# A decoder trunk on one core: later planner slots for the first scores of each pair of heads and for the norms' third block of transposes

## The chip, the cores and the metric

The kernel runs on one core of one Trainium2 chip. The metric is the device time of one execution in microseconds; the three runs of the kernel before lie between 1220.03 and 1221.92, with a median of 1221.85.

## The reference, cut to what matters

Two layers over a residual stream x of 512 tokens by 1024 features, all in float32:

```python
for l in range(2):
    h = x @ w_in[l]
    (fq, fk, fv, fgate, cq, ckv, kr, sq, sk, sv, wq, wk, wv) = split(h)
    out_a = causal_softmax(heads(fq), heads(fk), heads(fv), bias=cumsum(log_sigmoid(fgate + b)))
    out_b = mla(cq, ckv, kr, ...)            # low-rank q and kv, rotary key
    out_c = stick_breaking(heads(sq), heads(sk), heads(sv))
    out_d = sliding_window(heads(wq), heads(wk), heads(wv), sinks, slopes)
    y = group_rmsnorm(concat([out_a, out_b, out_c, out_d])) @ w_o[l]
    x = layernorm(ALPHA * x + y, ln1_g[l], ln1_b[l])
    f = (silu(x @ w_gate[l]) * (x @ w_up[l])) @ w_down[l]
    x = layernorm(ALPHA * x + f, ln2_g[l], ln2_b[l])
```

Each of the four groups has 4 heads of 64; the scores of groups A, B and C are causal, group D looks 128 tokens back.

## The kernel before, in words

The 512 tokens form four blocks of 128 (`NT` = 4, `t` from 0 to 3). x lies token by token (tile `x_res`); for the projections it is also held feature by feature (tile `xT`), which TensorE makes by transposing 128x128 pieces. Every float32 product is made as three products of a high and a low part (high x high, high x low, low x high), so operands exist in pairs: a high part, mostly a cast on ScalarE (L722, L453, L927), and a low part, the difference, on VectorE or GpSimd (L442, L444). One step over 128 of the summed features, with its three matmuls, is called a slice here; a projection chunk has eight. In the profile the weights' parts are named w_hi and w_lo, or qk where they borrow those buffers.

**How the order is made.** When the program is built, a planner (class `Sched`, L120 to L201) lays every operation out in estimated time. A generator asks for a slot with `Op(engine, cost, dep)`; `dep` holds, for each engine, the estimated time at which operands made there are done. The earliest start is the engine's free time or the operands' times plus a hand-over (`NEAR`), whichever is later. `pick` looks at all requests that wait for an engine, takes those whose start is within 30 ns (`SLACK`) of the earliest, and of these the one of the best priority. `mark(e, t)` makes a `dep` that says "ready on engine e at time t". The estimates set only the order in which each engine gets its instructions, and which PSUM bank or which of two engines is taken; on the chip each engine runs its list in that order, and semaphores make it wait for true operands. `sums` already asks for its slot 1500 ns behind its operand in this way.

**Scores.** `causal_group` (L1515 on) makes the heads of groups C, A and B. For each head h it makes three requests b = 0, 1, 2 through `head`: b = 0 is key blocks 0 and 1 (in the order, rows of 128x128, 128x256 and a mask row 128x2x128), b = 1 is 384 wide, b = 2 is 512 wide. All three read the same q and k (`operands(h)`). A pair of heads (0 and 1, 2 and 3) shares one q tile and one k tile. `head` asks for its score slot on TensorE and makes the scores; `normed` turns them into weights on ScalarE, VectorE and GpSimd; then come transposes of the weights (L1558), their evacuation to tile pt, and with the third the product with the values.

**Norms.** `layernorm` (L793 on) works through one token block t: statistics (L811 to L841, and L477 to L481 on tile lnst), a centred product (L854), and the final scale and shift in two halves of 512 columns (L859), all on VectorE. Ahead of them L1744 (first norm) or L2004 (second) adds the residual. When a half is done, `transpose_x(t, h, dep)` asks for four transposes of it on TensorE (L752); ScalarE and VectorE evacuate them to xT (L453, L442). The second norm of the last layer writes the output and transposes nothing, so there are three such places: the first norm of layer 0, its second norm, and the first norm of layer 1. While the last blocks are normed, TensorE has the next projection's slices for the first blocks to do. `load_x` uses `transpose_x` too, for the input.

Of the kernel before, what the change touches and what calls it, by code (L numbers as in the profile page):

```python
# [32 lines left out]
NT = S // P  # L33
# [32 lines left out]
E_PE, E_ACT, E_DVE, E_POOL, E_SP = range(5)  # L66
# [11 lines left out]
def join(*deps):  # L78

    if any(x is None for x in deps):  # L80
        return None
    return tuple(map(max, zip(*deps))) if len(deps) > 1 else deps[0]


def mark(e, t):
    return NOW[:e] + (t,) + NOW[e + 1:]
# [22 lines left out]
def c_mm(n):  # L109
    return max(107.0, 0.4225 * n)  # L110
# [9 lines left out]
class Sched:  # L120
# [9 lines left out]
    def spawn(self, gen, prio=0, order=None):  # L130
        self.n += 1
        self.step((gen, prio, self.n if order is None else order), None)
# [220 lines left out]
def trunk(ctx: ExitStack, tc: tile.TileContext, d):  # L353
# [43 lines left out]
    ident = const.tile([P, P], F32, name="ident")  # L397
    x = const.tile([P, NT, D], F32, name="x_res")
    x_dep = [None] * NT
# [7 lines left out]
    given = {"const": Joint(4)}  # L407
# [333 lines left out]
        return u, e  # L741


    def transpose_x(t, h, dep, then=None, keep=None):

        def half():
            yield lambda: r_u.ready()
            u = r_u.take()
            e = yield Op(E_PE, 4 * 107.0, join(u.dep, dep))
            for k in range(4):  # L750
                kk = h * 4 + k
                PE.transpose(out=u.tile[:, k * P:(k + 1) * P], in_=x[:, t, kk * P:(kk + 1) * P], identity=ident)  # L752
            tok = slice(t * P, (t + 1) * P)
            dst = [xt["t"][:, h * 4:h * 4 + 4, a, tok] for a in range(2)]
            e2 = yield from evac(dst, u.tile.rearrange("p (k n) -> p k n", k=4), S, join(e, xt["dep"]))
            if keep:
                e3 = yield from keep(h, tok, u.tile.rearrange("p (k n) -> p k n", k=4), e)
                u.give(join(e2, e3))
            else:
                u.give(e2)  # L760
            both = turned_x.setdefault(t, Joint(2))
            both.add(join(e, e2))
            if both.dep:
                xT_at[t] = turned_x.pop(t).dep
                if then:
                    then(t, both.dep)

        spawn(half())
# [98 lines left out]
    def layer(l):  # L867
# [602 lines left out]
        def mixf_ready(g, ticket):  # L1470
            return NOW if g in mixfs else mixf_turn.ready(ticket)

        def take_mixf(g):
            if g not in mixfs:
                mixfs[g] = mixf_turn.take()
# [39 lines left out]
        def causal_group(g, operands, extras, strict, normed, values, v_at, n_work, free_qk):  # L1515

            ticket = mixf_turn.ticket()
            heads = Joint(4, lambda dep: spawn(finish(g, dep)))
            extras = extras or (lambda h, i, o: [])

            def masks(o, b):

                if b == 0:
                    return o.rearrange("p (a n) -> p a n", a=2)[:, :, :P], identb, maskb[:, strict:strict + 1].broadcast_to([P, 2, P])
                return o[:, (b + 1) * P:(b + 2) * P], identb, maskb[:, strict]

            out = []
            for h in range(4):
                turned = Joint(3)
                pts = {}  # L1530
                pt_ticket = pt_turn.ticket()

                def head(b, ps, w, h=h, turned=turned, pts=pts, pt_ticket=pt_ticket):
                    blocks = ((0, 1), (1, 2)) if b == 0 else ((b + 1, b + 2),)
                    pairs, dep = operands(h)
                    cost = 108.0
                    for i, n in blocks:
                        cost += len(pairs) * c_mm(n * P)
                        for _, _, y in extras(h, i, ps.tile[:, :n * P]):
                            cost += max(54.0, 0.4225 * y.shape[-1])  # L1540
                    e = yield Op(E_PE, cost, join(dep, ps.dep, given["const"].dep))
                    c = 0
                    for i, n in blocks:
                        o = ps.tile[:, c:c + n * P]
                        qk_mm(o, pairs, i, n * P, c == 0, [masks(ps.tile, b)] * (c == 0) + extras(h, i, o))
                        c += n * P
                    free_qk(h, e)
                    p, end = yield from normed(ps, blocks, w, e)

                    yield lambda: join(r_u.ready(), NOW if pts else pt_turn.ready(pt_ticket))  # L1550
                    if not pts:
                        pts["pt"] = pt_turn.take()
                    pt = pts["pt"]
                    u = r_u.take()
                    n = 3 if b < 2 else 4
                    e = yield Op(E_PE, 107.0 * n, join(u.dep, end))
                    for k in range(n):
                        PE.transpose(out=u.tile[:, k * P:(k + 1) * P], in_=p.tile[:, k * P:(k + 1) * P], identity=ident)  # L1558
                    p.give(e)
                    e = join(e, pt.dep)  # L1560
                    e = yield from evac_blocks(pt.tile, u.tile, PIECES[b], e)
                    u.give(e)
                    turned.add(e)
                    if turned.dep is None:
                        return

                    ready = yield lambda: join(at[v_at].dep, r_u.ready(), mixf_ready(g, ticket)) if v_at in at else None
                    take_mixf(g)
                    v = v_of[values].tile
                    o = r_u.take()  # L1570
                    e = yield Op(E_PE, 2 * 600.0, join(turned.dep, ready, o.dep))
                    for kb in range(NT):
                        s0 = PLACE[kb] + kb
                        for part in range(2):
                            mm(o.tile[:, kb * P:], v[:, kb, h, :, :].rearrange("p a c -> p (a c)"),
                               pt.tile[:, part, s0 * P:(s0 + NT - kb) * P], start=(kb == 0 and part == 0), stop=False)
                    pt.give(e)
                    v_uses[values].add(e)
                    heads.add((yield from merge(o, g, h, e)))

                for b in range(3):
                    out.append((lambda h=h: operands(h) and operands(h)[1], n_work, lambda ps, w, b=b, head=head: head(b, ps, w)))
            return out
# [597 lines left out]
    def load_x(*ts):  # L2181
        def loads():
            for t in ts:
                x_dep[t] = yield from dma(x[:, t], d["x"][0, t * P:(t + 1) * P, :], 1.46)
                for h in range(2):
                    transpose_x(t, h, join(x_dep[t], given["ident"]), scale_x)
        return loads

    def first():
# [83 lines left out]
```

## Time and profile before

| | |
|---|---|
| median of three runs | 1221.85 us |
| profiled execution | 1222.01 us |
| its span | 1220.2 us (1.8 us lie around it) |
| TensorE busy | 1182.5 us, 7589 matmuls |
| VectorE, ScalarE, GpSimd busy | 896.0, 680.2, 247.6 us |
| mean granted TensorE clock | 0.992 |

How to read it: PE is TensorE, DVE VectorE, ACT ScalarE, POOL GpSimd. A row of the timeline has the start, the duration, engine, line, operation, and in brackets the engine's idle time before it with the operation that ended it. Neighbouring rows may be joined (x4 is four instructions), and matmuls overlap at their ends, so durations of neighbours add up to more than the time they take. A row of the table by stretches has the stretch, its length, busy time with the count of instructions for TensorE, its weight loads, VectorE, ScalarE and GpSimd, then the granted clock as a share of full speed, the share of DMA time and GB/s. In layer 0 the attention stage lies between some 40 and 236 us, the first norm about 236 to 270, the dense stage up to about 608, where the second norm lies; layer 1 has its first norm at about 840 to 873.

### The profile page before, as it was taken

How to read it: one execution, taken by the hardware profiler on the slowest of the kernel's cores; microseconds unless marked ns; L12 is line 12 of the kernel's file. 1: busy time of each engine (PE TensorE's matmuls, PEld its weight loads, DVE VectorE, ACT ScalarE, POOL GpSimd, SP SyncE). 2: the span in 40 equal slices, each digit the busy share in tenths (PEclk: the TensorE clock that was granted, in tenths of full speed). 3: DMA queues.
4: the chain of work that ended last, by engine and by line, in shares of the span. 5: the costliest groups of instructions: out<-in, count | busy, mean ns of one | idle time of the engine just before them, and what ended most of it. 6: DMA issues, size and time to landing. Idle time of an engine off the chain costs nothing.

```text
span 1220.2 us, 20174 instructions
## 1 busy us (share of the span) xinstructions
PE 1182.5 (97%) x7589; PEld 1069.7 (88%) x7589; DVE 896.0 (73%) x1699; ACT 680.2 (56%) x1434; POOL 247.6 (20%) x250
## 2 busy tenths in 40 slices
PE   9999999989999999999999999999999999999996
PEld 7988878789999989998789788787899989899985
DVE  5679668799986648872665786788998956499626
ACT  4769759456654335552346788684665634256421
POOL 3552764400000000000035536643000000000001
PEclk9999999999999999999999999999899999999999
DMA  6322230423333143323233121303234341332341
GB/s 201 88 57 53 57 104 1 139 79 89 96 109 106 61 138 96 113 88 121 86 71 86 43 75 31 104 25 115 87 88 120 93 134 50 108 119 88 104 138 70
DMA packets 112162, 110.75 MB, mean 91 GB/s; under 512 B 9792, under 2 KB 94656, under 8 KB 112064
## 3 DMA queue, kind: packets, MB, share of 16 engines
q1 hardware_dynamic: 112064, 109.45, 30.0%
q8 instruction: 60, 0.98, 0.3%
q14 instruction: 38, 0.31, 0.1%
HBM read 107.34 MB, written 2.10 MB: 90 GB/s over the span
## 4 chain that ended last, share of the span: by engine, by line
PE 77%; DVE 10%; ACT 6%; issue 3%; POOL 2%; DMA 1%; SPq 0%; POOLq 0%; DVEq 0%; ACTq 0%
PE ps L464 75%; POOL w_lo L442 2%; PE ps L1558 2%; DVE qk L442 1%; DVE x_res L1744 1%; DVE pt L442 1%; DVE x_res L859 1%; DVE xT L442 1%; DMA x_res<-in_x 1%; ACT xT L722 0%; PE ps L752 0%; ACT temp L1446 0%; DVE qk L444 0%; DVE temp L1307 0%; DVE augk L1093 0%
## 5 line engine op out<-in xcount | busy, mean ns | idle before, releaser
L464 PE MATMUL ps<-xT,w_hi 128*128 128x256 f32 (+1 forms) x1128 | 215.7, 319 | 0.0
L464 PEld LDWEIGHTS ps<-xT,w_hi 128*128 128x128 f32 x1128 | 162.5, 191 | 11.5
L464 PE MATMUL ps<-w_hi,qk 128*128 128x512 f32 (+1 forms) x560 | 170.9, 387 | 0.0
L464 PE MATMUL ps<-xT,w_lo 128*128 128x256 f32 (+1 forms) x888 | 166.2, 305 | 1.2 <-POOL w_lo L442 1.2
L722 ACT CAST w_hi<-w_raw 128x1024 fp32r<-128x1024 f32 (+2 forms) x86 | 87.9, 1024 | 111.4 <-PE ps L464 88.7
L442 POOL TENSOR_TENSOR w_lo<-w_raw,w_hi 128x1024 fp32r<-128x1024 f32 (+4 forms) x66 | 121.6, 1850 | 89.1 <-ACT w_hi L722 72.4
L442 DVE TENSOR_TENSOR w_lo<-w_raw,w_hi 128x1024 fp32r<-128x1024 f32 x47 | 57.6, 1226 | 111.6 <-ACT w_hi L722 111.5
L464 PEld LDWEIGHTS ps<-xT,w_lo 128*128 128x128 f32 x888 | 123.7, 191 | 9.4 <-POOL w_lo L442 2.0
L464 PEld LDWEIGHTS ps<-w_hi,qk 128*128 128x128 f32 x560 | 104.2, 188 | 20.8
L464 PE MATMUL ps<-w_hi,mix 128*128 128x512 f32 x352 | 110.8, 396 | 3.7 <-DVE x_res L1744 1.9
L464 PE MATMUL ps<-w_lo,qk 128*128 128x512 f32 (+1 forms) x280 | 108.1, 386 | 0.0
L1912 ACT COPY temp<-ps 128x256 f32<-128x256 f32 x120 | 44.5, 371 | 85.3 <-PE ps L464 84.8
L773 POOL TENSOR_SCALAR x_res<-x_res 128x1024 f32<-128x1024 f32 x8 | 8.8, 1106 | 373.9 <-DVE lnst L841 357.1
L659 ACT CAST w_hi<-temp 128x512 fp32r<-128x512 f32 x78 | 48.3, 620 | 64.6 <-DVE temp L602 35.4
L464 PEld LDWEIGHTS ps<-w_hi,mix 128*128 128x128 f32 x352 | 65.8, 190 | 17.3 <-DVE x_res L1744 2.4
L467 POOL TENSOR_TENSOR lnst<-lnst,mhalf 128x1 f32<-128x1 f32 x4 | 3.9, 984 | 363.3 <-DVE lnst L841 363.3
L442 DVE TENSOR_TENSOR w_hi<-temp,w_hi 128x512 fp32r<-128x512 f32 x78 | 53.4, 689 | 30.6 <-ACT w_hi L659 30.4
L659 ACT CAST w_lo<-temp 128x512 fp32r<-128x512 f32 x82 | 50.7, 620 | 42.8 <-DVE temp L602 27.9
L464 PE MATMUL ps<-xT,qk 128*128 128x256 f32 x528 | 69.5, 292 | 2.0 <-DVE qk L442 2.0
L464 PE MATMUL ps<-w_lo,mix 128*128 128x512 f32 x176 | 69.7, 396 | 1.8 <-POOL w_lo L442 1.8
L464 PEld LDWEIGHTS ps<-xT,qk 128*128 128x128 f32 x528 | 67.2, 200 | 2.8 <-DVE qk L442 2.7
L464 PE MATMUL ps<-w_hi,xT 128*128 128x388 f32 (+1 forms) x256 | 68.9, 350 | 0.4 <-DVE qk L444 0.4
(234 smaller groups left out, 2700.8 us busy)
## 6 DMA issues: line engine op xcount, KB each, us to landing
w_raw<-in_w_down SPq DMA_DIRECT2D x44, 512.0 KB, 3.8
w_raw<-in_w_in SPq DMA_DIRECT2D x26, 512.0 KB, 3.7
w_raw<-in_w_gate SPq DMA_DIRECT2D x24, 512.0 KB, 3.6
w_raw<-in_w_up SPq DMA_DIRECT2D x24, 512.0 KB, 3.7
w_raw<-in_w_o SPq DMA_DIRECT2D x16, 512.0 KB, 3.6
vd<-in_w_up SPq DMA_DIRECT2D x10, 512.0 KB, 3.8
mixf<-in_w_up SPq DMA_DIRECT2D x10, 512.0 KB, 3.7
vd<-in_w_gate SPq DMA_DIRECT2D x10, 512.0 KB, 4.5
```

The source lines that it names most:

```text
L442: eng.tensor_tensor(out=lo, in0=src, in1=f(hi), op=ALU.subtract)
L464: PE.matmul(out, lhsT=lhsT, rhs=rhs, start=start, stop=stop, skip_group_check=True)
L467: POOL.tensor_tensor(out=out, in0=ve, in1=mhalf[:ve.shape[0], :ve.shape[1]], op=ALU.pow)
L659: ACT.copy(out=self.part[0], in_=src)
L722: ACT.copy(out=out, in_=in_ if psum is None else psum)
L773: POOL.tensor_scalar(out=x[:, t], in0=x[:, t], scalar1=ALPHA, scalar2=0.0, op0=ALU.mult, op1=ALU.add)
L859: DVE.scalar_tensor_tensor(out=x[:, t, csl], in0=centred[c], scalar=st[:, 9:10], in1=bb[c], op0=ALU.mult, op1=ALU.add)
L1558: PE.transpose(out=u.tile[:, k * P:(k + 1) * P], in_=p.tile[:, k * P:(k + 1) * P], identity=ident)
L1744: DVE.scalar_tensor_tensor(out=x[:, t, csl], in0=ps.tile, scalar=rs[:, t:t + 1], in1=x[:, t, csl], op0=ALU.mult, op1=ALU.add, accum_out=st ...
L1912: ACT.copy(out=dst, in_=src)
```

## The change

`transpose_x` gets an argument `late`, true except for the input's transposes. For the third token block (`t == NT - 2`) the slot of its four transposes, in both halves, is asked for 1500 ns after the latest estimated time of its operands. In `head`, the first block of scores (b = 0) of an even head is asked for 1000 ns after the latest estimated time of q and k. The operations and their true operands stay as they were; the instruction counts are the same.

```diff
-    def transpose_x(t, h, dep, then=None, keep=None):
+    def transpose_x(t, h, dep, then=None, keep=None, late=True):
 
         def half():
             yield lambda: r_u.ready()
             u = r_u.take()
-            e = yield Op(E_PE, 4 * 107.0, join(u.dep, dep))
+
+            e = yield Op(E_PE, 4 * 107.0, join(u.dep, mark(E_DVE, max(dep) + 1500.0) if late and t == NT - 2 else dep))
...
+                    if h % 2 == 0 and b == 0:
+                        dep = mark(E_DVE, max(dep) + 1000.0)
                     e = yield Op(E_PE, cost, join(dep, ps.dep, given["const"].dep))
...
-                    transpose_x(t, h, join(x_dep[t], given["ident"]), scale_x)
+                    transpose_x(t, h, join(x_dep[t], given["ident"]), scale_x, late=False)
```

Lines after the first edit are one higher in the changed kernel, after the second three.

Three places of the new order. First TensorE in layer 1 at the scores of C head 0: ps..._7442 (7438 in the change) is the chunk of the next projection, qk0 and qk6 are k and q, ps6_7458 (ps6_7455) the first block of scores, ps1_7461 (ps4_7458) the second, kh0 the high part of k; the rows with ones are the sums for the norm of group D. Before:

```order
L464 MATMUL ps7_7442<-xT_6482,w_hi1_7245 128x512 x2
L464 MATMUL ps7_7442<-xT_6482,w_lo1_7246 128x512
L464 MATMUL ps6_7458<-qk0_7441,qk6_7378 128x128
L464 LDWEIGHTS identb_74
L464 MATMUL ps6_7458<-maskb_77,identb_74 128x2x128
L464 MATMUL ps6_7458<-kh0_69,qk6_7378 128x128
L464 MATMUL ps6_7458<-qk0_7441,qk6_7378 128x256
L464 MATMUL ps6_7458<-kh0_69,qk6_7378 128x256
L464 MATMUL ps1_7461<-qk0_7441,qk6_7378 128x384
```

The change:

```order
L464 MATMUL ps3_7438<-xT_6482,w_hi1_7245 128x512 x2
L464 MATMUL ps3_7438<-xT_6482,w_lo1_7246 128x512
L464 MATMUL ps7_7428<-ones_75,temp1_7392 128x1 x4
L464 MATMUL ps4_7458<-qk0_7437,qk6_7388 128x384
L464 LDWEIGHTS identb_74
L464 MATMUL ps4_7458<-maskb_77,identb_74 128x128
L464 MATMUL ps4_7458<-kh0_69,qk6_7388 128x384
L464 MATMUL ps3_7438<-xT_6482,w_hi1_7245 128x512 x2
L464 MATMUL ps3_7438<-xT_6482,w_lo1_7246 128x512
L464 MATMUL ps6_7455<-qk0_7437,qk6_7388 128x128
```

The second block now stands first, and the first block one slice behind it. Of the chunk, four slices stood ahead of the scores before, and two stand there now, with a group of four ones.

Second, TensorE in the first norm of layer 0, at the transposes of the third block (x_res as input); ps7_2872 (ps4_2872) is the end of the chunk before, ps6_2928 (ps5_2919) the next chunk, qk0 its weights' high part, qk1 their low part. Before:

```order
L464 MATMUL ps7_2872<-xT_2683,qk8_2682 128x256
L752 MATMUL ps2_2907<-ident_72,x_res_73 128x128 x4
L752 MATMUL ps4_2915<-ident_72,x_res_73 128x128 x4
L464 MATMUL ps6_2928<-xT_2683,qk0_2707 128x256 x2
L464 MATMUL ps6_2928<-xT_2683,qk1_2708 128x256
```

The change:

```order
L464 MATMUL ps4_2872<-xT_2683,qk8_2682 128x256
L753 MATMUL ps7_2907<-ident_72,x_res_73 128x128 x4
L464 MATMUL ps5_2919<-xT_2683,qk0_2707 128x256 x2
L464 MATMUL ps5_2919<-xT_2683,qk1_2708 128x256
L753 MATMUL ps1_2911<-ident_72,x_res_73 128x128 x4
```

The first half's transposes stand where they stood; the second half's follow one slice later. The first norm of layer 1 has the same change; in the second norm of layer 0 the third block's transposes don't move.

Third, VectorE in the second norm of layer 0, at the fourth block; xT rows are evacuations of transposes (ps..._6613, 6651 and 6654 those of the blocks before, ps3_6709 or ps1_6683 the fourth block's first half), qk0 and qk3 the low parts of the next two chunks' weights, L859 (L860) the norm's last operation. Before:

```order
L442 TENSOR_TENSOR xT_6482<-ps6_6651,xT_6482 128x4x128
L479 TENSOR_SCALAR lnst2_6369<-lnst2_6369 128x1
L442 TENSOR_TENSOR xT_6482<-ps2_6654,xT_6482 128x4x128
L481 TENSOR_SCALAR lnst2_6369<-lnst2_6369 128x1
L442 TENSOR_TENSOR qk0_6634<-w_raw0_6493,qk4_6633 128x1024
L859 SCALAR_TENSOR_TENSOR x_res_73<-x_res_73,lnst2_6369,vd0_6371 128x512
L442 TENSOR_TENSOR qk3_6701<-w_raw1_6505,qk1_6700 128x1024
```

The change:

```order
L481 TENSOR_SCALAR lnst2_6369<-lnst2_6369 128x1
L442 TENSOR_TENSOR xT_6482<-ps5_6651,xT_6482 128x4x128
L860 SCALAR_TENSOR_TENSOR x_res_73<-x_res_73,lnst2_6369,vd0_6371 128x512
L442 TENSOR_TENSOR xT_6482<-ps7_6654,xT_6482 128x4x128
L860 SCALAR_TENSOR_TENSOR x_res_73<-x_res_73,lnst2_6369,vd0_6371 128x512
L442 TENSOR_TENSOR qk0_6634<-w_raw0_6493,qk4_6633 128x1024
L442 TENSOR_TENSOR xT_6482<-ps1_6683,xT_6482 128x4x128
```

Both last operations of the fourth block now stand ahead of the low part qk0. On TensorE the fourth block's transposes stand after five and seven slices of the first chunk, where they stood after two and seven slices of the second.

## The prediction

> **What bounds the kernel now.** First the page: its busy times and the chain that ended last.
>
> ```profile
> PE 1182.5 (97%) x7589; PEld 1069.7 (88%) x7589; DVE 896.0 (73%) x1699; ACT 680.2 (56%) x1434; POOL 247.6 (20%) x250
> PE 77%; DVE 10%; ACT 6%; issue 3%; POOL 2%; DMA 1%; SPq 0%; POOLq 0%; DVEq 0%; ACTq 0%
> ```
>
> TensorE works for 1182.5 of the 1220.2 us of the span. No instruction is added or removed, so its work is the same afterwards; what the change can win or lose lies in the other 37.7 us and in the clock. Next the waits of TensorE (total in us, times, longest), of which the largest names what one half of the change aims at:
>
> ```profile
> PE ps L752 <- DVE x_res L859: 5.4, 4, 2.1
> ```
>
> Then the timeline of TensorE at these places: the third block's transposes in the first norm of layer 0, in the second norm of layer 0 and in the first norm of layer 1, then the first scores of the pairs that wait (C heads 0 of both layers, C head 2 and A head 2 of layer 1).
>
> ```profile
> 259.76 0.63 PE L752 MATMUL ps<-ident,x_res 128*128 128x128 f32 x4 [1.30 <-DVE x_res L859]
> 261.10 0.63 PE L752 MATMUL ps<-ident,x_res 128*128 128x128 f32 x4 [0.71 <-DVE x_res L859]
> 261.48 0.48 PE L464 MATMUL ps<-xT,qk 128*128 128x256 f32 x2
> 262.39 1.01 PE L464 MATMUL ps<-xT,qk 128*128 128x256 f32 x3 [0.42 <-DVE qk L442]
> 610.79 0.66 PE L752 MATMUL ps<-ident,x_res 128*128 128x128 f32 x4 [2.15 <-DVE x_res L859]
> 611.73 0.63 PE L752 MATMUL ps<-ident,x_res 128*128 128x128 f32 x4 [0.28 <-DVE lnst L841]
> 616.78 0.74 PE L464 MATMUL ps<-xT,qk 128*128 128x256 f32 x4 [1.32 <-DVE qk L442]
> 864.39 0.63 PE L752 MATMUL ps<-ident,x_res 128*128 128x128 f32 x4 [1.27 <-DVE x_res L859]
> 865.17 0.63 PE L752 MATMUL ps<-ident,x_res 128*128 128x128 f32 x4 [0.15 <-DVE lnst L833]
> 78.16 0.33 PE L464 MATMUL ps<-qk,qk 128*128 128x128 f32 x1 [0.49 <-POOL qk L724]
> 683.02 0.30 PE L464 MATMUL ps<-qk,qk 128*128 128x128 f32 x1 [1.23 <-DVE qk L442]
> 706.72 0.33 PE L464 MATMUL ps<-qk,qk 128*128 128x128 f32 x1 [1.22 <-ACT qk L722]
> 773.97 0.33 PE L464 MATMUL ps<-qk,qk 128*128 128x128 f32 x1 [0.55 <-ACT qk L722]
> ```
>
> The transposes wait 1.30 + 0.71 + 2.15 + 0.28 + 1.27 + 0.15 = 5.86 us, the scores 0.49 + 1.23 + 1.22 + 0.55 = 3.49 us. Were every such wait filled with other work, 9.35 us would be won directly.
>
> Last the clock, in stretches of one clock window (3.41 us), with TensorE's busy time and the granted clock (1.00 or 0.50):
>
> ```profile
> 255.39:258.80 3.41, 3.07 (x25) 2.83 (x24) 3.41 (x11) 1.85 (x5) 0.00 (x0) 1.00 0.00 0
> 258.80:262.21 3.41, 1.50 (x10) 1.11 (x10) 3.41 (x8) 1.96 (x6) 0.00 (x0) 1.00 0.00 0
> 262.21:265.63 3.42, 3.24 (x15) 3.25 (x16) 3.42 (x11) 1.33 (x5) 0.00 (x0) 0.50 0.52 153
> 811.76:815.17 3.41, 2.50 (x20) 1.83 (x18) 3.03 (x11) 3.36 (x10) 1.73 (x4) 1.00 0.01 2
> 815.17:818.59 3.42, 3.42 (x15) 2.84 (x14) 1.75 (x5) 3.27 (x7) 2.80 (x3) 0.50 0.01 2
> ```
>
> A quiet window is followed by one at half clock. At half clock 15 matmuls fit into 3.42 us; at full clock 25 took 3.07, so 28 would fit. Such a window costs 3.42 x (1 - 15/28) = 1.6 us of matmul time, call it 1.5. The rows at 811.76 show that "quiet" isn't "idle": TensorE was busy for 2.50 of 3.41 us, with transposes and products with a vector of ones only, and half clock followed.
>
> The Trainium skill, "TensorE: Matmul & The Clock Gate", under "Why this matters for your kernels", asks only that no idle gap exceed some 3 us; by that none of these places would be throttled, and the 1.5 us would not exist. The trace has gaps of at most 2.15 us and throttles, so the rows decide; its "Part 4: PE-mode transpose", that transposes don't count as busy in the same way, is borne out.
>
> **The change part by part.** *First scores.* Only the first of a head's three blocks (b = 0) gets the later time. The second block reads the same q and k and has the old time, so the planner puts it into the slot that is left: the order shows this for C head 0 and A head 2 in both layers and for A head 0 in layer 0. A wait for q and k therefore stays and changes its owner: 0.49 and 0.55 stay, at 0.
>
> For C head 0 of layer 1 the slot moves as well: two slices of the next projection and a group of ones lie ahead of it, where four slices did. The timeline prices both, by the starts of successive rows:
>
> ```profile
> 684.12 0.63 PE L464 MATMUL ps<-xT,w_hi 128*128 128x512 f32 x2
> 684.82 0.63 PE L464 MATMUL ps<-xT,w_hi 128*128 128x512 f32 x2
> 686.19 0.95 PE L464 MATMUL ps<-ones,temp 128*128 128x1 f32 x8
> 686.99 0.72 PE L464 MATMUL ps<-xT,w_hi 128*128 128x512 f32 x2
> ```
>
> A slice is 0.70 us, a group of eight ones 0.80, of four 0.4. The lead falls from 2.8 to 1.8 us, and the wait of 1.23 would grow by 1.0 to 2.2 if q and k came as late as before. But they were late for a reason of their own, on VectorE and GpSimd:
>
> ```profile
> 672.45 0.54 DVE L1093 TENSOR_SCALAR augq<-temp,amask 128x512 fp32r<-128x512 f32 x1
> 674.98 2.74 DVE L1093 TENSOR_SCALAR augk<-temp,amask 128x512 fp32r<-128x512 f32 x1
> 675.03 2.40 POOL L442 TENSOR_TENSOR w_lo<-w_raw,w_hi 128x1024 fp32r<-128x1024 f32 x1 [8.96 <-ACT w_hi L722]
> ```
>
> One kind of operation took 0.54 us, and 2.74 beside a GpSimd subtraction: 2.2 us lost, behind which the group's last products, ScalarE's scaling and then k's copies queued. VectorE's order here changes. If the two miss each other, the wait is as in layer 0, 0.49; if not, 2.2. Between these I take the 1.2 of before: 0, from -0.74 to +1.0.
>
> C head 2 of layer 1 keeps its first block first, but in another PSUM bank. Its 1.22 waits for ScalarE's copy out of the bank, not for q and k; the new bank was released long before. I take -1.22; at worst 0.
>
> *What follows in layer 0's attention.* The product of values and weights of A head 1 comes two slices and two groups later, with its evacuations ahead of the others, so its two waits should go, -0.88 (0 at worst):
>
> ```profile
> 157.59 0.50 PE L464 MATMUL ps<-pt,v 128*128 128x512 f32 x1 [0.62 <-ACT pt L1364]
> 158.35 0.50 PE L464 MATMUL ps<-pt,v 128*128 128x512 f32 x1 [0.26 <-DVE pt L442]
> ```
>
> A head 0's scores come 1.3 us of TensorE work earlier and didn't wait: +0.3, between 0 and the 0.55 of A head 2.
>
> *Norms, first norm of both layers.* The first of the two transposes keeps its place, so 1.30 and 1.27 stay. The second goes behind one slice. VectorE's order there is unchanged, and that is what decides:
>
> ```profile
> 260.20 0.75 DVE L859 SCALAR_TENSOR_TENSOR x_res<-x_res,lnst,lnv 128x512 f32<-128x512 f32 x1
> 261.11 1.22 DVE L442 TENSOR_TENSOR qk<-w_raw,qk 128x1024 fp32r<-128x1024 f32 x1
> 266.56 1.42 DVE L859 SCALAR_TENSOR_TENSOR x_res<-x_res,lnst,lnv 128x512 f32<-128x512 f32 x2
> 267.37 0.66 PE L752 MATMUL ps<-ident,x_res 128*128 128x128 f32 x4
> 267.78 0.96 PE L464 MATMUL ps<-xT,qk 128*128 128x256 f32 x6
> ```
>
> The slice needs the low part that VectorE finishes at 262.33, a full operation after the second transpose's input (260.95). So the slice's first two matmuls run at about 260.4, its third waits till 262.39 as it does now, and the second transpose, ready long before, follows it. Its 0.41 us (267.37 to 267.78) leaves a wait and lands on work: +0.4 in each layer, +0.8. Queued behind it are ScalarE's and VectorE's copies of it; VectorE has its copy behind the low part and two more products of the norm in its order, so nobody else waits. There is cover, too: the fourth block's transposes start at 267.37, just when VectorE's input for them is done (266.56 and one operation of 0.75, as at 260.20). If TensorE gets there early, it waits; then the 0.4 costs nothing, and a half-clock window saved here brings only what VectorE allows.
>
> *Second norm of layer 0.* The third block's transposes don't move; 2.15 and 0.28 stay. Their later times push other things: VectorE does the fourth block's two last operations before the low part, and the fourth block's transposes move up into the first projection, after five and seven slices. The rows that lay it out:
>
> ```profile
> 611.50 0.21 DVE L841 TENSOR_SCALAR lnst<-lnst 128x1 f32<-128x1 f32 x1
> 614.14 0.68 DVE L442 TENSOR_TENSOR xT<-ps,xT 128x512 fp32r<-128x512 f32 x1
> 612.11 3.35 PE L464 MATMUL ps<-xT,qk 128*128 128x256 f32 x26
> ```
>
> From 611.7 VectorE has two 512-wide operations, three short ones, two copies and one operation to do before the fourth block's first half is ready: with 0.7 (half of 1.42) for an operation of the norm, 0.65 for a copy (0.68 less a little overlap) and 0.1 for a short one, 3 x 0.7 + 2 x 0.65 + 0.3 = 3.7, so 615.4. The second half follows after a copy and an operation at 616.7, the low part after 1.2 at 617.9. TensorE has done five slices (15 matmuls of 3.35/26 us) from 612.11 at 614.0 and stops for 1.4 us there, where it stopped for 1.32 ahead of 616.78; two more slices of 0.36 then stand before the second half, one behind it, and the second projection's third matmul, which stood at 616.78, at about 617.9. By then 0.8 us of transposes (two times 0.41) are done which before stood behind 616.78: 617.9 - 616.8 - 0.8 = +0.3, between -0.3 and +0.6 for the steps' errors.
>
> *Clock.* Quiet stretches stay about as long: in the first norms two matmuls of the slice stand between two waits, as now. 0, with 1.5 either way for each window.
>
> Sum: -1.22 - 0.88 + 0.3 + 0.8 + 0.3 = -0.7. The profiled execution took 1222.01, so 1221.3; the median of the runs is 0.16 lower: 1221.2. The 0.2% that a measurement of this kernel can tell from no change are 2.4 us; this is within.
>
> **The rivals.** *Faster: the re-dealt scores find their operands.* For it: ScalarE instead of GpSimd makes the high part of k in layer 1, and the collision at 674.98 is one order away from vanishing. Then C head 0 gains 0.74, A head 0 loses nothing (-0.3), the 0.49 and 0.55 go (-1.04), the norms' 0.8 is hidden behind VectorE and the second norm comes out at -0.3 instead of +0.3 (0.6): 3.5 less, 1217.7; with one half-clock window fewer, such as that at 815, 1216.2. Against it: the second block's need for the same q and k. Chance 0.38.
>
> *Slower: a collision of VectorE and GpSimd on the way to the scores.* The trace has another such case, where the next product stood 1.74 us:
>
> ```profile
> 176.66 2.88 DVE L442 TENSOR_TENSOR qk<-temp,qk 128x512 fp32r<-128x512 f32 x1
> 181.10 0.70 PE L464 MATMUL ps<-w_hi,mix 128*128 128x512 f32 x2 [1.74 <-DVE xT L442]
> ```
>
> In layer 1 the operation of 674.98 now stands directly ahead of k's low part on VectorE, and the lead is shorter. If GpSimd's subtraction starts inside it, C head 0 loses 1.0; the stage behind it slips, so that C head 2's 1.22 stays, and one more collision in the new order costs another 1.74: 1221.2 + 1.0 + 1.22 + 1.74 = 1225.2. It decides once GpSimd's operation overlaps by over 1.8 us, the new lead. For it: two such collisions in one execution; against it: most GpSimd operations meet no such partner. Chance 0.22.
>
> *The change doesn't do what it says* (the waits stay where they are) is the core of the forecast, and another phase of the clock windows moves it by 1.5 at a time. Chance 0.40.
>
> **How the numbers follow.** 1221.2 with 0.40. Downwards the range takes in the faster case with a second window saved, 1214.7, say 1215; upwards the slower case and some 0.8 of the norms' and windows' spread, 1226. Over 0.2% faster 0.38, within 0.40, slower 0.22.
>
> **What would show it.** Right: the second block of the scores waiting about 0.5 us at C head 0 of layer 0; 1.3 us ahead of the third block's first transpose in both first norms, and the slice's third matmul still waiting for VectorE's low part; a wait of the fourth block's transposes near 614; no wait at C head 2 of layer 1 and none at 157. Wrong: the sum of waits for x_res (5.4) halved, or the first score of C head 0 of layer 1 waiting under 0.3 or over 2 us; or a count of half-clock windows that differs by two.

## The result, and the profile after

The changed kernel took 1231.55 us (median of six runs, 1225.95 to 1234.14), the kernel before 1221.71 (six runs, 1220.03 to 1221.92). The ratio is 1.0073, with a 95% interval of 1.0058 to 1.0088: slower by 0.7%, about 9 us, where 1221.2 and no change were forecast. The profiled execution took 1233.63 us, its span is 1231.9. One execution of all that follow, in the run with extra matmuls in the norms (6), took 1291.92 us at a mean granted clock of 0.848; the ratio there leaves it out.

The page of the change: busy times, then the chain that ended last.

```profile
PE 1186.9 (96%) x7589; PEld 1076.5 (87%) x7589; DVE 896.1 (73%) x1699; ACT 685.9 (56%) x1437; POOL 242.2 (20%) x247
PE 82%; DVE 10%; ACT 3%; issue 3%; POOL 1%; DMA 0%; POOLq 0%; DVEq 0%; SPq 0%; ACTq 0%
```

Of the 11.7 us between the two spans, 4.4 are TensorE busier with the same 7589 matmuls (1186.9 against 1182.5; more of them ran at half clock), and 7.3 are time in which it did nothing (45.0 against 37.7). Four rows of the waits of TensorE in the change (total, times, longest):

```profile
PE ps L753 <- DVE x_res L860: 5.7, 4, 2.2
PE ps L464 <- ACT qk L722: 5.0, 1, 5.0
PE ps L464 <- DVE xT L442: 3.5, 2, 1.8
PE ps L464 <- ACT qk L455: 1.4, 1, 1.4
```

What the norms' half aimed at, the wait for x_res, went from 5.4 to 5.7. One wait of 5.0 us is new. The timeline shows it and the other places that answer to those shown of before: C head 0 of layer 0, the first norm of layer 0 with a stall 30 us behind it, the second norm of layer 0, then C head 0 of layer 1 and two places behind it.

```profile
79.06 0.44 PE L464 MATMUL ps<-qk,qk 128*128 128x384 f32 x1 [0.49 <-POOL qk L724]
258.37 0.63 PE L753 MATMUL ps<-ident,x_res 128*128 128x128 f32 x4 [1.30 <-DVE x_res L860]
258.75 0.48 PE L464 MATMUL ps<-xT,qk 128*128 128x256 f32 x2
260.99 0.58 PE L464 MATMUL ps<-xT,qk 128*128 128x256 f32 x1 [1.75 <-DVE qk L442]
261.37 1.05 PE L753 MATMUL ps<-ident,x_res 128*128 128x128 f32 x4
289.09 1.10 PE L464 MATMUL ps<-v,w_hi 128*128 128x256 f32 x7 [0.95 <-DVE w_hi L442]
612.14 0.66 PE L753 MATMUL ps<-ident,x_res 128*128 128x128 f32 x4 [2.15 <-DVE x_res L860]
616.74 0.63 PE L753 MATMUL ps<-ident,x_res 128*128 128x128 f32 x4 [0.96 <-DVE x_res L860]
687.33 0.69 PE L464 MATMUL ps<-qk,qk 128*128 128x384 f32 x1 [4.97 <-ACT qk L722]
764.50 0.50 PE L464 MATMUL ps<-qk,w_hi 128*128 128x512 f32 x1 [1.41 <-ACT qk L455]
793.27 0.70 PE L464 MATMUL ps<-w_hi,mix 128*128 128x512 f32 x2 [1.75 <-DVE xT L442]
```

The first five rows are as forecast: the second block of scores (128x384) has taken over the 0.49, the first transpose of the third block waits 1.30 as before, and the slice's third matmul waits for VectorE's low part. The 4.97 was 1.23 before.

For the rest of the text the execution is cut at five marks that can be read off such rows: A from the third block's first transpose in layer 0's first norm to the same in its second norm; B from there to the first score of C head 0 in layer 1; C from there to the third block's first transpose in layer 1's first norm; D from there to the end. Before, for example, A is 610.79 - 259.76. In brackets stands how many windows of half clock (3.41 us) lie in the stage, by the record of the granted clock; the stretch of half clock at the very end of every execution is not counted. The change was run and profiled a second time (7); its row shows what only the windows moved.

| kernel | start to A | A | B | C | D | span |
|---|---|---|---|---|---|---|
| before | 259.76 (0) | 351.03 (1) | 72.23 (0) | 181.36 (2) | 355.84 (1) | 1220.2 |
| the change | 258.37 (2) | 353.77 (2) | 75.20 (0.2) | 185.20 (2.8) | 359.32 (2) | 1231.9 |
| the change again | 258.25 (1) | 352.14 (0) | 75.23 (1.8) | 183.47 (1.2) | 359.21 (2) | 1228.3 |
| scores part alone | 258.00 (1) | 351.02 (0) | 71.83 (1) | 183.97 (2) | 356.51 (0) | 1221.3 |
| norms part alone | 260.19 (1) | 352.13 (0) | 75.23 (1.8) | 183.42 (2.2) | 359.23 (2) | 1230.2 |
| second norm alone | 260.55 (1) | 351.03 (1) | 75.24 (0.4) | 187.21 (4.6) | 356.88 (1) | 1230.9 |
| first norms alone | 260.77 (0) | 352.64 (1) | 72.32 (1) | 179.67 (0) | 357.93 (1) | 1223.3 |

The loss isn't in one place: against before, the change is 1.4 us shorter up to A, and 2.7 longer in A, 3.0 in B, 3.8 in C and 3.5 in D. A and D begin in the first norms; B runs from the second norm to C head 0 of layer 1, and C through the rest of that layer's attention.

### The profile page after: what moved, and what is told of

It reads as the page before. It is cut to its first block, busy times and chain, and to the rows that moved or that the text cites. A ratio compares the mean times of both kernels' runs of the same rounds, so it can differ in the third digit from the quotient of the medians.

```text
span 1231.9 us, 20175 instructions
## 1 busy us (share of the span) xinstructions
PE 1186.9 (96%) x7589; PEld 1076.5 (87%) x7589; DVE 896.1 (73%) x1699; ACT 685.9 (56%) x1437; POOL 242.2 (20%) x247
## 4 chain that ended last, share of the span: by engine, by line
PE 82%; DVE 10%; ACT 3%; issue 3%; POOL 1%; DMA 0%; POOLq 0%; DVEq 0%; SPq 0%; ACTq 0%
PE ps L464 79%; PE ps L1561 2%; DVE x_res L1747 1%; POOL w_lo L442 1%; DVE qk L442 1%; PE ps L753 1%; DVE xT L442 1%; DVE x_res L860 1%; DVE pt L442 1%; ACT xT L722 0%; DVE temp L1308 0%; DMA x_res<-in_x 0%; DVE qk L444 0%; DVE x_res L855 0%; DVE mix L444 0%
## 5 line engine op out<-in xcount | busy, mean ns | idle before, releaser
L464 PEld LDWEIGHTS ps<-xT,w_hi 128*128 128x128 f32 x1128 | 163.2, 192 | 11.2
L722 ACT CAST w_hi<-w_raw 128x1024 fp32r<-128x1024 f32 (+2 forms) x93 | 94.4, 1016 | 113.1 <-PE ps L464 85.1
```

The source lines that it names most:

```text
L464: PE.matmul(out, lhsT=lhsT, rhs=rhs, start=start, stop=stop, skip_group_check=True)
L722: ACT.copy(out=out, in_=in_ if psum is None else psum)
```

## The experiments

Three theories were tried. **A**: the loss sits at C head 0 of layer 1, where k comes late because ScalarE now copies k's high part and takes turns with VectorE, with half clock behind that wait; that VectorE's operations stretch beside GpSimd's was added to it in experiment 4. **B**: the first norms lose it, to longer quiet stretches and half clock. **C**: the scores' new order loses it, by the shorter lead and a collision of VectorE and GpSimd.

**1. The scores part alone.**

```diff
-            e = yield Op(E_PE, 4 * 107.0, join(u.dep, mark(E_DVE, max(dep) + 1500.0) if late and t == NT - 2 else dep))
+            e = yield Op(E_PE, 4 * 107.0, join(u.dep, dep))
```

> Scores part alone: the norms' transposes get their old slots back, the first scores keep the later one. In the order k's high part at C head 0 of layer 1 is copied by GpSimd, as before the change. Theory A (the loss is the 4.97 us wait there, because ScalarE makes that copy and takes turns with VectorE at one PSUM bank, plus the half-clock windows behind it): wait at C head 0 of layer 1 at most 2.2 us, median 1220 to 1223. Theory B (the norms' second transposes behind a slice lengthen the quiet stretch and cost half-clock windows): 1220 to 1223 as well, and both first norms as before. Theory C (the shorter lead and the collision of VectorE and GpSimd, both of the scores' order): wait over 3 us again, median 1226 or more.

1221.46 us, ratio 1.0005 (0.9996 to 1.0014), and 1.23 us of wait at C head 0 of layer 1. Theory C has fallen: four slices stand ahead of C head 0 here, as before, so the shorter lead, too, comes with the norms' half. This half does what was forecast in sum, but not stage by stage: up to the first norm it wins 1.8 us, and C gives 2.6 back.

**2. The norms part alone.**

```diff
-                    if h % 2 == 0 and b == 0:
-                        dep = mark(E_DVE, max(dep) + 1000.0)
```

> Norms part alone: the first scores get their old slots back, so four slices stand ahead of C head 0 of layer 1, but ScalarE still makes the copy of k's high part there. Theory A: the wait there is 3 to 4 us (4.97 less the 1.0 of lead), median 1226 to 1230. Theory B: wait about 1.2 us as before, both first norms with one or two half-clock windows behind them, median 1225 to 1228. Theory C: wait about 1.2 us and median 1221 to 1224.

1231.98 us, ratio 1.0098 (1.0082 to 1.0113): the whole loss, and more than theory A said (1226 to 1230, with a wait of 3 to 4 us). The wait at C head 0 of layer 1 is there, 4.97 us, 75 us behind the second norm of layer 0:

```profile
687.55 0.47 PE L464 MATMUL ps<-qk,qk 128*128 128x128 f32 x1 [4.97 <-ACT qk L722]
```

So it is the norms' slots, not the scores', through which the planner comes to another state and gives k's high part to ScalarE.

**3. Its two halves.** The later slot in the second norm of layer 0 only, and in the first norms only (from the kernel of experiment 2):

```diff
-            transpose_x(t, c, dep, keep=keep)
+            transpose_x(t, c, dep, keep=keep, late=False)
```

> The later slot only in the second norm of layer 0; both first norms and all scores as before. In the order ScalarE copies k's high part at C head 0 of layer 1, as in the change. Theory A (the wait there, with the half-clock windows behind it, and layer 1's re-dealt attention carry the loss): wait 4.97 again, median 1226 to 1230. Theory B (the first norms carry it): wait there, but median 1222 to 1225.

```diff
-                transpose_x(t, c, dep, scale_x)
+                transpose_x(t, c, dep, scale_x, late=False)
```

> The later slot only in the first norms of both layers; twelve rows of TensorE's order differ from before, all at these norms. Theory A: 1.1 us in each layer (measured in the runs without half-clock windows there), median 1222.5 to 1224. Theory B: two half-clock windows more in each of most runs, median 1225 to 1228.

The second norm alone took 1232.06 us (ratio 1.0083, 1.0070 to 1.0096) with a wait of 4.98 at C head 0; the first norms alone 1225.55 (1.0041, 1.0029 to 1.0053). So the later slot in the second norm is enough for the wait and for a loss as large as the whole (2 us above what A said); theory A holds for the larger part. B has a share, larger than A expected, and here not for the reason it gave: layer 0's first norm in this run has one half-clock window, as before. In the change B's reason adds to it: A has two windows and takes 353.77 us, and 352.14 with none when run again, so they cost 1.6. The rows of the first norms alone:

```profile
263.39 0.58 PE L464 MATMUL ps<-xT,qk 128*128 128x256 f32 x1 [1.75 <-DVE qk L442]
263.76 1.05 PE L753 MATMUL ps<-ident,x_res 128*128 128x128 f32 x4
290.37 2.90 PE L464 MATMUL ps<-v,w_hi 128*128 128x256 f32 x22 [0.95 <-DVE w_hi L442]
```

The last row is a stall in the dense stage, 30 us behind the norm, in both layers; the kernel before has none there. VectorE's order is the same up to the low part for which the slice waits, and another behind it, where it prepares the dense stage's first weights. The parts don't add up (0.4 + 4.7 + 11.2 against 9.8): each leads the planner to another order behind it, and the clock's windows fall differently in each.

**4. What makes k late at C head 0 of layer 1.** VectorE and GpSimd there, in the change:

```profile
674.70 2.00 DVE L1089 TENSOR_TENSOR temp<-temp,augq 128x512 f32<-128x512 f32 x1
680.27 2.86 DVE L1096 SCALAR_TENSOR_TENSOR augq<-temp,amask,augq 128x512 fp32r<-128x512 f32 x1
683.87 1.00 DVE L1094 TENSOR_SCALAR augk<-temp,amask 128x512 fp32r<-128x512 f32 x1
684.90 1.05 DVE L1096 SCALAR_TENSOR_TENSOR augk<-temp,amask,augk 128x512 fp32r<-128x512 f32 x1
685.99 0.68 DVE L442 TENSOR_TENSOR qk<-ps,kh 64x512 fp32r<-64x512 f32 x1
687.92 0.69 DVE L442 TENSOR_TENSOR qk<-ps,kh 64x512 fp32r<-64x512 f32 x1 [1.25 <-ACT qk L722]
```

```profile
673.12 3.03 POOL L442 TENSOR_TENSOR w_lo<-w_raw,w_hi 128x1024 fp32r<-128x1024 f32 x1 [9.67 <-ACT w_hi L722]
679.75 2.83 POOL L442 TENSOR_TENSOR w_lo<-w_raw,w_hi 128x1024 fp32r<-128x1024 f32 x1
683.23 3.29 POOL L1104 TENSOR_SCALAR augh<-augq,amask 128x512 fp32r<-128x512 f32 x4 [0.65 <-DVE augq L1096]
```

Two of VectorE's operations end 0.55 us behind the GpSimd subtraction beside them (676.70 after 676.15, 683.13 after 682.58), and those beside GpSimd's third row take 1.0 us. The Trainium skill, "SBUF — State Buffer", "SBUF: two separate sides", has it that a VectorE operation with two inputs in SBUF and a GpSimd operation that reads SBUF take one pair of ports whole, in turn; the two ends agree. ScalarE adds to it: its copy of k's high part reads the same bank as VectorE's low part, and they run in turns:

```profile
686.70 1.18 ACT L722 CAST qk<-ps 64x512 fp32r<-64x512 f32 x2 [5.28 <-DVE qk L442]
```

ScalarE, free since k's first copies, waits 5.28 us for VectorE's first half, and VectorE's second half 1.25 for ScalarE. The Trainium skill's "PSUM — Partial Sum Buffer", "PSUM bank collisions raise a hardware error", says that two engines' accesses to one bank and the same 32 partitions are kept apart by a dependency; the two waits fit, since each half's low and high part read the same 64 rows.

Three runs took these apart. First the copy by GpSimd instead of ScalarE:

```diff
+                if l == 1 and name == ("sk", 0):
+                    e = yield Op(E_POOL, c_pool(S), join(a[i], k.dep))
+                    POOL.tensor_scalar(out=k.tile[64 - i * 64:128 - i * 64, i], in0=f(kh.tile[row, i]), ...)
```

> The whole change, with one copy (k's high part at C head 0 of layer 1) given to GpSimd instead of ScalarE. Theory A: the wait of 4.97 falls to 2.2 or less, the two half-clock windows behind it go, median 1224 to 1227 (what is left are the norms). Theory B: the wait falls, but the median stays at 1227 to 1230. Theory C: wait over 3 us, median within 1.5 us of the change's.

Then GpSimd's two subtractions left out:

```diff
+            c.cut = l == 1 and col in (SK + P, FQ)
...
+                    if getattr(self, 'cut', False):
+                        ACT.activation(out=lo[:, cs], in_=raw[:, cs], func=AF.Copy, scale=0.0)
```

> The whole change in its own order, but two of GpSimd's subtractions in layer 1 (the low parts of the weights of the second k chunk of group C and of the first q chunk of group A, which overlap VectorE ahead of C head 0) are left out: ScalarE writes zeros there instead, so those low parts are missing from the products. Theory A (VectorE is late at C head 0 because its operations stretch beside these two subtractions): VectorE's operations between 674 and 686 us take 0.4 to 0.75 us each instead of up to 2.86, the wait of 4.97 falls below 2.0, and the time from the second norm's transposes to C head 0 from 75.2 to about 72. Rival (the order alone makes VectorE late): the wait stays over 4 us.

Then both, with the copy's place in the plan kept:

> The whole change in its own order, with the two GpSimd subtractions left out as above (those low parts are zero) and k's high part at C head 0 of layer 1 copied by GpSimd instead of ScalarE, in the same place of the plan. If VectorE's stretched operations and the turn-taking at the bank are two separate halves of the 4.97 us wait: it falls below 1.0, since each alone took it to 2.4 to 2.5. If they are the same delay seen twice: it stays at about 2.4.

The first score of C head 0 in these three, in this order; of the first also the two slices that now stand ahead of it:

```profile
678.72 0.72 PE L464 MATMUL ps<-xT,w_hi 128*128 128x512 f32 x2
679.28 0.40 PE L464 MATMUL ps<-xT,w_lo 128*128 128x512 f32 x1
679.52 0.62 PE L464 MATMUL ps<-xT,w_hi 128*128 128x512 f32 x2
679.98 0.40 PE L464 MATMUL ps<-xT,w_lo 128*128 128x512 f32 x1
682.80 0.41 PE L464 MATMUL ps<-qk,qk 128*128 128x384 f32 x1 [2.43 <-DVE qk L442]
```

```profile
683.60 0.45 PE L464 MATMUL ps<-qk,qk 128*128 128x384 f32 x1 [2.53 <-ACT qk L725]
```

```profile
682.77 0.41 PE L464 MATMUL ps<-qk,qk 128*128 128x384 f32 x1 [1.72 <-DVE qk L442]
```

Each alone takes the wait from 4.97 to about 2.5, both to 1.72; all three are above what was said of a cause that explains the wait (2.2, 2.0 and 1.0 at most). But the wait by itself misleads in the first run: moving the copy there also put two slices, 1.5 us of work, ahead of the score. What counts is when the score starts, which is B: 74.18, 72.92 and 71.94 us, where the change has 75.20, the change again 75.23, and the kernel before 72.23. So the copy by ScalarE costs 1.0 us and the two subtractions 2.3, and both together 3.3: in this measure the two causes add up, and without them k is no later than before. Of the 3.74 us by which the wait grew, 3.0 are k's delay and 0.8 the shorter lead (71.00 us from the norm's mark to the end of the work ahead before, 70.22 in the change). Without the two subtractions VectorE's operations there are mostly back at 0.4 to 0.75 us, but one still takes 1.79 beside another GpSimd operation.

The times are 1228.94 (1.0065, 1.0051 to 1.0079), 1227.81 (1.0054, 1.0041 to 1.0067) and 1227.28 us (1.0036, 1.0022 to 1.0050). The first is above what theory A said (1224 to 1227): with the wait halved, most of the loss is still there. By B the late k is worth about 3 us of it; the rest is elsewhere.

**5. ScalarE's copy in the kernel before.** The same branch as in the first of the three, in the kernel before, with `E_ACT` and a copy out of `ps`.

> The kernel before, with k's high part at C head 0 of layer 1 copied by ScalarE out of PSUM instead of GpSimd out of SBUF. If the turn-taking of ScalarE and VectorE at the bank costs by itself: the wait of 1.23 grows by one copy of 0.6 to about 1.85; if it is the wait for VectorE's whole queue that makes 4.97, the queue must be as late as in the change, and it grows only where VectorE's order changes too. Median 1221 to 1224 by the first; a wait over 4 us and 1225 or more if ScalarE's copy alone carries the 3.7 us.

```profile
683.31 0.33 PE L464 MATMUL ps<-qk,qk 128*128 128x128 f32 x1 [1.74 <-ACT qk L940]
758.12 0.51 PE L464 MATMUL ps<-qk,w_hi 128*128 128x512 f32 x1 [1.41 <-ACT qk L455]
786.87 0.47 PE L464 MATMUL ps<-w_hi,mix 128*128 128x512 f32 x1 [1.74 <-DVE xT L442]
```

The turn-taking alone costs about what was expected: 1.74 us of wait where 1.85 was said. But the run took 1225.18 us (1.0039, 1.0026 to 1.0051), 4.3 more than before and above the 1221 to 1224 expected with such a wait, because moving this one copy re-deals layer 1's attention behind it: the waits of 1.41 and 1.74 are those of the change, and the kernel before has neither in layer 1. Stage C takes 182.00 us here with no half clock in it, and 179.67 in the order of before with none (first norms alone): 2.3 us for the order. Runs with the same order as before agree on the last figure: the scores part in layer 0 only (8) takes 179.67 in C as well, with none.

**6. Half clock in the norms.** Extra matmuls of constants in the waits of the kernel before, ahead of the third and fourth block's transposes:

```diff
+            n_fill = 3 if fill and t >= NT - 2 else 0
             e = yield Op(E_PE, 4 * 107.0, join(u.dep, dep))
+            for k in range(n_fill):
+                mm(u.tile[:, :2 * P], identb, maskb.rearrange("p a n -> p (a n)"), start=True, stop=True)
```

> The kernel before, with three extra matmuls (bf16, 128x256, of constants, into the bank that the transposes then overwrite) ahead of each group of four transposes of the third and fourth block in the three norms; 0.1 us each at full clock, all else in the same order. If half clock follows a window with too few ordinary matmuls, transposes not counting: no half-clock window within 10 us after the third block's transposes, mean clock 0.994 or more, median 1218 to 1221, since most of the fillers stand in waits. If it follows idle time of whatever kind: windows as before, median 1222 to 1225.

No half-clock window follows the third block's transposes in the profiled run. That doesn't settle what brings half clock, since the scores part alone has none behind them in either first norm, without extra matmuls: the windows' phase may do it. The time is no better, 1223.17 us (1.0018, 1.0008 to 1.0027), where 1218 to 1221 was expected; what the full clock won is lost again at once:

```profile
263.83 3.13 PE L464 MATMUL ps<-xT,qk 128*128 128x256 f32 x24 [0.48 <-DVE qk L442]
268.15 0.74 PE L464 MATMUL ps<-xT,qk 128*128 128x256 f32 x4 [1.19 <-DVE qk L442]
```

The 1.19 us of wait ahead of 268.15 stands just behind the place of the half-clock window of before. The table says it without extra matmuls: A takes 351.03 us with a window in the norm (before) and 351.02 with none (scores part alone), and D 355.84 with one (before) and 355.83 with none (scores part in layer 0 only). So in the order of before, VectorE sets the pace behind the third block's transposes. It isn't so in every order: in the change two windows there cost 1.6 us (A, 353.77 against 352.14), and one cost 0.6 (352.70, the run without the two subtractions).

Nor is it so a few us earlier. In C the kernel before has two windows, at 815 and 856, and takes 1.7 us longer than the first norms alone, which have the same order there and no window. Nearly all of it lies at 856, between the transposes of the second and the third block in layer 1's first norm; the kernel before, then the first norms alone:

```profile
853.72 0.66 PE L752 MATMUL ps<-ident,x_res 128*128 128x128 f32 x4 [0.43 <-DVE lnst L811]
```

```profile
856.24 0.66 PE L753 MATMUL ps<-ident,x_res 128*128 128x128 f32 x4 [0.44 <-DVE lnst L812]
865.40 0.63 PE L753 MATMUL ps<-ident,x_res 128*128 128x128 f32 x4 [1.36 <-DVE x_res L860]
```

From the second to the third block's transposes it is 10.67 us before (853.72 to 864.39) and 9.16 here (856.24 to 865.40): 1.5 us for one window. The one at 815 is worth 0.2 at most.

**7. Half clock behind the 4.97 us wait.** 36 extra matmuls ahead of C head 0's scores in the change, and the change again beside it:

```diff
+                    for _ in range(36 if l == 1 and g == GC and h == 0 and b == 1 else 0):
+                        mm(ps.tile[:, :2 * P], identb, maskb.rearrange("p a n -> p (a n)"), start=True, stop=True)
```

> The whole change, with 36 extra matmuls of constants (bf16, 128x256, some 0.1 us each, 3.9 us in all) in TensorE's order just ahead of the first scores of C head 0 of layer 1, where it waits 4.97 us; they go into the bank that the scores then overwrite. If half clock behind this wait costs time because TensorE sets the pace there: no half-clock window within 10 us behind C head 0, the scores start when they did, and the kernel is 1.5 to 3 us faster than the change in the same job. If TensorE has to wait for others there anyway, as in the norms: no such window, but the median within 0.7 us of the change's.

> The change itself once more, as the measure for the run with the extra matmuls and for the spread: 1226 to 1234, with the time rising as the mean granted clock falls from 0.994 to 0.985, some 0.7 us for each us of clock lost.

1228.05 us with them (1227.06 to 1232.48, five runs), 1230.20 without (1226.68 to 1234.06, six). No half-clock window follows C head 0 in the profiled run, but the spreads overlap nearly whole, and that run has two windows near 764 which the change's profiles have not. The medians differ by 2.2 us, and nothing is shown by it.

**8. Later slots where they help.** The scores part in layer 0 only; then there for all three blocks of the even heads; then that in both layers. Norms as before in all three.

```diff
-                    if h % 2 == 0 and b == 0:
+                    if l == 0 and h % 2 == 0 and b == 0:
```

> The scores part in layer 0 only; layer 1 and all norms in the order of before. In the run with the whole scores part, layer 0 up to the first norm took 1.76 us less than before although one half-clock window more fell into it, and layer 1's attention gave 2.6 back. If these are effects of the order: 1217.5 to 1219.5, faster by 2 to 3 us. If layer 0's gain was the first load's timing or the clock's phase: 1220 to 1222, no change.

```diff
-                    if l == 0 and h % 2 == 0 and b == 0:
+                    if l == 0 and h % 2 == 0:
```

> The scores part in layer 0 only, as in the run that was faster, but with the later slot for all three blocks of the even heads instead of the first alone; three slices instead of two stand ahead of C head 0. If the forecast's step holds that the second block takes over the wait because it has the old slot: the wait of 0.50 at C head 0 of layer 0 is gone here, and the median is within 1 us of 1217.9. If the wait has another owner, it stays at 0.5.

```diff
-                    if l == 0 and h % 2 == 0:
+                    if h % 2 == 0:
```

> All three blocks of the even heads later, now in both layers; norms as before. In the order C head 0 of layer 1 has five slices of the next chunk ahead of it, where four stood before and two in the change. If later slots for whole heads help in layer 1 as in layer 0 (5 us less there, up to the first norm): 1210 to 1214. If layer 1's re-dealt attention gives it back, as with the first block alone: 1215 to 1219.

1217.94 us (ratio 0.9975, 0.9967 to 0.9984), 1215.40 (0.9954, 0.9943 to 0.9966) and 1214.23 (0.9937, 0.9924 to 0.9949): all three beat both kernels. C head 0 of layer 0 with the first block alone, and with all three:

```profile
79.12 0.44 PE L464 MATMUL ps<-qk,qk 128*128 128x384 f32 x1 [0.50 <-POOL qk L724]
```

```profile
78.71 0.40 PE L464 MATMUL ps<-xT,w_lo 128*128 128x512 f32 x1
78.94 0.29 PE L464 MATMUL ps<-qk,qk 128*128 128x128 f32 x1
```

With all three blocks late the wait is gone, so the second block's old slot was what kept it. The time was expected within 1 us of 1217.9 there and came out 2.5 lower; what else the order won is open. In the last of the three, layer 1 gains as well (C 178.31 us with one half-clock window, where the order of before takes 179.67 with none; the wait at its C head 0 is 0.57 us), less than layer 0 did (254.27 us up to A against 259.76).

## Why the prediction was wrong, point by point

- **First scores: right.** The second block took over the wait (0.49 at the 128x384 row), all blocks late removed it (8), and this part alone changed nothing that can be measured (1). Stage by stage it did more than forecast, both ways (1).
- **C head 2 of layer 1 and A head 1 of layer 0: right.** Neither the 1.22 at C head 2 nor the 0.62 and 0.26 at 157 is among the change's waits; the wait put at 0.3 for A head 0 isn't either.
- **C head 0 of layer 1: the step that failed.** The sum took 0, between -0.74 and +1.0, and set the wait between 0.49 and 2.2. It was 4.97, +3.74: the lead fell as foreseen (by 0.8), but k, taken to come as late as before, came 3.0 us later. The prediction had one collision of VectorE and GpSimd in hand and asked whether it would stay or go; there were two long ones and two short ones ahead of k, and the two subtractions cost 2.3 us (4). And it read ScalarE's copy of k's high part as a relief, a point for "faster", where that copy waits its turn behind VectorE and costs 1.0 (4).
- **What lies behind it: no term.** The sum stopped at C head 2. The rest of layer 1's attention was re-dealt: C is 3.8 longer in the profiled run with 2.8 half-clock windows, 2.1 when run again with 1.2, and 2.3 in a like order with none against none (5). The scores part alone, which leaves the wait as it was, loses 2.6 in C too, so this term belongs to both halves of the change. The rival "slower" had the right place and one of the causes for the wait but reached only 1225.2, since it lacked this, the copy and the norms.
- **First norms: the right mechanism at the wrong size.** The first transpose stayed, the slice's third matmul waited (1.75), the second transpose came behind it. Forecast +0.4 each; A is 1.1 longer with no half clock in either (norms part alone 352.13, scores part alone 351.02). D has no half clock in the run with GpSimd's copy and takes 357.62, 1.1 more than the scores part alone (356.51), whose norm is as before. VectorE's order was compared only up to the low part; behind it lies the 0.95 at the dense stage, which the sum lacked. Half clock comes on top: 1.6 for two windows in A, 1.7 for two in D (359.32 against 357.62).
- **Second norm: right where it stands** (0.96 of wait at the fourth block where 1.4 was worked out; with it alone B is 3.0 longer, less than the 3.7 by which the wait at its end grew, so nothing is lost ahead of that wait), wrong in that the account was closed there: this is the edit whose after-effects are enough for a loss as large as the whole (3).
- **Clock: one price for every window, and the same number of them.** "0, 1.5 either way" per window: 1.5 is right for the one at 856, but those behind the third block's transposes cost nothing in the order of before and 1.6 for two in the change's (6). Nor does the row at 811.76 show by itself that transposes don't count as busy, since products with a vector of ones lie in it too. And the change has nine in its body (without the end) where before has four. Its six runs go from 1225.95 us at a mean granted clock of 0.994 to 1234.14 at 0.985. The fastest is 5.9 us above the fastest of before: that much is order and waits at the least; the other 4 of the median go with the clock.

So the sum missed by four terms, none of which it had in this size: k's delay (B, 3.0), the re-dealt attention (C, 2.3 in a like order without half clock), the first norms (1.1 each where 0.4 stood), and the half-clock windows. Left open: why the planner's later state re-deals layer 1's attention to the worse; what sets the number of windows; and what each costs behind C head 0.

## What to carry to other kernels

A slot moved in a list scheduler moves everything planned after it: cost the change to the end of the program, place by place. Where one of several users of an operand is told to come later, another takes the slot and the wait; delay them all, as the two fastest versions here do. When a copy changes its engine in the new order, ask whose turn it now waits for. To price a delay, compare when the late operand's first user starts; the wait ahead of it also changes with the work that stands there.

## What the runs showed of the hardware

- A half-clock window, which takes 1.7 us of clock (half of 3.41), has no price of its own: none behind the third block's transposes in the order of before (351.03 us with, 351.02 without), 1.5 between the second and third block's in layer 1 (10.67 against 9.16), 1.6 for two in the change (353.77 against 352.14).
- The same program runs at 0.994, 0.989 or 0.985 mean granted clock, 8 us apart (the change); the kernel before, in fourteen runs beside experiment 8, between 0.995 and 0.989, 4.3 us apart.
- A VectorE operation of 0.7 us took 2.0 to 2.9 us beside a GpSimd subtraction and ended 0.55 us after it.
- ScalarE and VectorE reading one PSUM bank took turns half by half, which made the first score start 0.5 us later in the order of before (72.75 against 72.23) and 1.0 in the change's (75.20 against 74.18).
